# A two-layer hybrid trunk on one core: block-diagonal 128 by 128 products of the recurrent mixer rewritten as 64 by 64 products

## The chip, the cores and the metric

The kernel runs on one core of one Trainium2 chip. The metric is the device time of one execution in microseconds (us), as the median of several runs. The core has the matrix engine (TensorE, PE in the profile, with its weight loads listed apart as PEld), the vector engine (DVE), the scalar engine (ACT), GpSimd (POOL) and SyncE (SP), which here only starts transfers.

## The reference, cut to what matters

A trunk of two layers over 512 tokens of width 1024, all in float32. Layer 0 has a recurrent mixer of two kinds of heads, layer 1 block attention; both layers have an MLP and a gated side input. The change is in the second kind of heads of layer 0's mixer, eight heads of width 64 that carry a 64 by 64 state from token to token:

```python
def rwkv7_scan(r, decay, k, v, kk, a):
    def step(state, inp):
        r_t, w_t, k_t, v_t, kk_t, a_t = inp
        sa = jnp.einsum('bhvk,bhk->bhv', state, -kk_t)
        state = (state * w_t[:, :, None, :]
                 + sa[..., None] * (kk_t * a_t)[:, :, None, :]
                 + v_t[..., None] * k_t[:, :, None, :])
        return state, jnp.einsum('bhvk,bhk->bhv', state, r_t)
```

## The kernel before, in words

The two heads of a pair lie in the two halves of the 128 partitions, so there are four pairs (`hp`, 0 to 3). The kernel doesn't step through tokens. It cuts the 512 tokens into eight chunks of 64 and handles them in two groups (`g`) of four chunks; a group is two blocks (`a`) of two chunks (`c_`). For a pair and a group it does, in this order:

- `p1`: scores inside each chunk (line 600): the keys of one chunk as stationary operand, the queries of that chunk as moving operand. So that one product serves both heads, the keys are first copied by ACT into `BH`, a 128 by 128 tile that holds the two heads' 64 by 64 blocks on its diagonal and zeros elsewhere (line 596). DVE multiplies the products by a triangular mask into `NA` and `KA` (line 605). Then four transposes per block (line 614), whose results ACT copies into `TOK` and, one chunk at a time, into the halves of `BZ`, again with zeros around (line 619). Two further products (lines 625 and 631) follow.
- `p2`: a chain of products in float16 (line 664) that inverts a triangular matrix by doubling, each step waiting for a copy by ACT or DVE; it ends in `MU` (lines 690 and 693).
- `p3`: the maps of the state over one chunk. For each block one product with 256 moving columns (line 707) and two accumulated pairs with 128 (lines 710 and 711). DVE takes the map out of PSUM into `GB` (line 714), ACT the added state into `HS` (line 718). Then a chain over chunks (`states`, lines 744 and 746), woven with two products that use 64 columns of the array (`inner`, lines 726 and 731).

Steps are generators. `step` strings them together: in "A" `p2(h, 0)` is woven with the rest, in "C" `p2(h, 1)` is woven with `p3(h, 0)` and the next pair's `pre`. The large projections (`gemm`, lines 244 to 246, three products per operand pair) are written between them. All of it is put in order when the program is built, by a scheduler that sees priorities (`run` raises them by `OFS`). So what stands behind what in an engine's queue isn't read from the source but from the built program.

PSUM tiles of the mixer come from the ring `pmr` of four banks. Products with float32 operands appear in the profile as two passes each, with a weight load each: the 64 products of line 600 are 128 instructions there. The projections' operands are split beforehand into two float32r parts, and their products are one pass each.

Of the kernel before, what the change touches and what calls it, by code (L numbers as in the profile page):

```python
# [185 lines left out]
def trunk(ctx, tc, wts, xT, pT, vecs, lora, cst, lev, seg, rope, gain, out, upto="all", dbg=None, mode=None):  # L186
# [177 lines left out]
    def layer0_mixer(actp):  # L364
        ph = ExitStack()
        mp = ph.enter_context(tc.tile_pool(name="mp", bufs=1))
        BH = mp.tile([P, 2, 4, P], F32, name="BH")
        NAs = [mp.tile([P, 2, 2, 2, P], F32, name=f"NA{i}") for i in range(2)]
        KAs = mp.tile([P, 2, 2, 2, P], F32, name="KA")
        BZ = [mp.tile([P, 2, 2, 2, P], F32, name=f"BZ{i}") for i in range(2)]  # L370
        GB = mp.tile([P, 4, P], F32, name="GB")
        SB = mp.tile([P, 9, P], F32, name="SB")
        PP = mp.tile([P, 4, P], F16, name="PP")
        early = [BH, KAs, *NAs, *BZ, GB, SB, PP]
        for t in early[:NE]:
            G.memset(t, 0.0)
        nc.gpsimd.dma_start(cs, cst[:, :NKEEP])
# [206 lines left out]
            yield  # L584

        pk = [(a, h) for a in range(2) for h in range(2)]

        def p1(hp, g):
            lw, bh, kh, ar, rh_, bo, dl, v, y = pre_[hp]
            gs = slice(g * 256, g * 256 + 256)  # L590
            NA, KA, TOK = NAs[g], KAs, []
            un[hp, g] = (NA, TOK)

            for n, (src, dst) in enumerate(((bh, NA), (kh, KA))):
                for h in range(2):
                    A.copy(BH[hs[h], n, :, hs[h]], src[hs[h], gs].rearrange("p (c t) -> p c t", t=64))
                ps = pmr.tile([P, S], F32, name="pmr")
                for c_ in range(4):
                    o = g * 256 + c_ * 64
                    T.matmul(ps[:, c_ * P:c_ * P + P].rearrange("p (x t) -> p x t", x=2), BH[:, n, c_, :],  # L600
                             ar[:, :, o:o + 64], start=True, stop=True)
                pv = ps.rearrange("p (a c x t) -> p a c x t", a=2, c=2, x=2)
                for h in range(2):
                    for c_ in range(2):
                        V.tensor_tensor(dst[hs[c_], :, h, :, hs[c_]], pv[hs[h], :, c_, :, :],
                                        tri[hs[h], None, :, :].to_broadcast([64, 2, 2, 64]), op=OP.mult)
                yield
            for a in range(2):
                j = 2 * g + a
                js = slice(j * P, j * P + P)  # L610

                ps = pmr.tile([P, S], F32, name="pmr")
                for n, src in enumerate((ar[:, 0, :], v, bh, kh)):
                    T.transpose(ps[:, n * P:n * P + P], src[:, js], ident)
                t = E("TOK", 4, [P, 3, P])
                pv = ps.rearrange("p (x f) -> p x f", x=4)
                A.copy(t[:, 0:2, :], pv[:, 0:2, :])
                for c_ in range(2):
                    A.copy(BZ[g][hs[c_], a, :, c_, :], pv[hs[c_], 2:4, :])
                TOK.append(t)  # L620
                yield

            ps = pmr.tile([P, S], F32, name="pmr")
            for i, (a, h) in enumerate(pk):
                T.matmul(ps[:, i * 64:i * 64 + 64], KA[:, a, h, 0, :], TOK[a][:, 1, hs[h]], start=True, stop=True)
            for a in range(2):
                A.copy(TOK[a][:, 2, :], ps[:, a * P:a * P + P])
            yield
            ps = pmr.tile([P, S], F32, name="pmr")
            for i, (a, h) in enumerate(pk):  # L630
                T.matmul(ps[hs[h], a * P:a * P + P], TOK[a][:, 1, hs[h]], KA[:, a, h, 1, :], start=True, stop=True)
            A.copy(y[:, gs], ps[:, :256])
            yield
# [64 lines left out]
        def p3(hp, g):  # L698
# [2 lines left out]
            gs = slice(g * 256, g * 256 + 256)  # L701

            HS = E("HS", 1, [P, 4, 64])
            for a in range(2):
                bz = BZ[g][:, a]
                ps = pmr.tile([P, S], F32, name="pmr")
                T.matmul(ps[:, :256], MU[:, a, 0, :], bz[:, 0].rearrange("p c f -> p (c f)"), start=True, stop=True)
                for c_ in range(2):
                    o = ps[:, 256 + c_ * P:256 + c_ * P + P]
                    T.matmul(o, bz[:, 0, c_, :], MU[:, a, 1, :], start=True, stop=False)  # L710
                    T.matmul(o, bz[:, 1, c_, :], TOK[a][:, 1, :], start=False, stop=True)
                pv = ps.rearrange("p (x c f) -> p x c f", x=2, c=2)
                for h in range(2):
                    V.tensor_tensor(GB[hs[h], 2 * a:2 * a + 2, hs[h]], pv[hs[h], 0, :, hs[h]],
                                    cc("istack")[hs[h], None, :].to_broadcast([64, 2, 64]), op=OP.add)
                    for c_ in range(2):
                        ch = 4 * g + 2 * a + c_
                        A.activation(HS[hs[h], 2 * a + c_, :], pv[hs[h], 1, c_, hs[h]], AF.Copy,
                                     scale=dl[hs[h], ch:ch + 1])
                yield  # L720


            def inner():
# [618 lines left out]
```

## Time and profile before

| what | value |
|---|---|
| median of 3 runs | 1512.53 us (1509.21 to 1513.5) |
| the profiled execution | 1513.45 us |
| its span, first to last instruction | 1511.7 us |
| PE busy | 1484.5 us, 98% of the span |
| DVE, ACT, POOL busy | 932.4, 663.0, 137.9 us |
| mean granted TensorE clock | 0.993 |

The profile is one execution; its time is 0.92 us above the median, and its span leaves out 1.75 us ahead of the first and behind the last instruction. A busy PE isn't a full PE: the profile counts a matmul from its start to its modelled end, and matmuls overlap. What a product costs PE is read from the distance between starts. Layer 0's mixer with its projections lies from about 17 to 440 us.

### The profile page before, as it was taken

The numbers are of one execution on the slowest core, as the hardware profiler recorded it, in microseconds if no ns is written. First come the engines' busy times: TensorE is split into PE (matmuls) and PEld (weight loads), VectorE is DVE, ScalarE is ACT, GpSimd is POOL, SyncE is SP. The second block draws the span as 40 slices with busy tenths as digits, with TensorE's granted clock in tenths as the row PEclk, the third lists the DMA queues.
The fourth block names the chain that finished last, engine by engine and source line by source line (L and its number), as shares of the span: only waits on it lengthen the run. The fifth ranks groups of instructions, "written<-read, shape, count | busy, mean of one in ns | idle before, by whom it ended". The sixth has DMA issues, their size and how long they took to land.

```text
span 1511.7 us, 20553 instructions
## 1 busy us (share of the span) xinstructions
PE 1484.5 (98%) x7578; PEld 1199.8 (79%) x7578; DVE 932.4 (62%) x1831; ACT 663.0 (44%) x1269; POOL 137.9 (9%) x133
## 2 busy tenths in 40 slices
PE   9999999999999999999999999999999999999998
PEld 7678787777677888888888888777778888888887
DVE  6878697687775664444446648477575444445463
ACT  4575555554436433333334534454634333333342
POOL 4121220310205000000000200000220000000000
PEclk9999999999999999999999999999999999999999
DMA  5110111201123233333333432221123333333331
GB/s 179 56 36 22 55 43 44 67 29 49 36 91 105 91 98 98 98 98 94 97 96 98 131 115 83 78 63 49 55 79 97 92 104 98 98 95 95 98 98 70
DMA packets 67110, 123.88 MB, mean 82 GB/s; under 512 B 7633, under 2 KB 8017, under 8 KB 67009
## 3 DMA queue, kind: packets, MB, share of 16 engines
q1 hardware_dynamic: 65376, 118.57, 25.8%
q10 hardware_dynamic: 1152, 2.43, 0.5%
q0 software_dynamic: 480, 1.57, 0.3%
q8 instruction: 59, 0.97, 0.3%
q14 instruction: 43, 0.34, 0.1%
HBM read 120.45 MB, written 2.10 MB: 81 GB/s over the span
## 4 chain that ended last, share of the span: by engine, by line
PE 90%; DVE 5%; ACT 3%; issue 2%; DMA 1%; POOL 0%; SPq 0%; ACTq 0%; DVEq 0%; POOLq 0%
PE pj L244 21%; PE pj L246 20%; PE pj L245 20%; PE pmr L245 1%; PE pmr L246 1%; PE pmr L244 1%; PE pmr L1268 1%; PE pmr L1244 1%; PE pmr L664 1%; PE pj L1171 1%; PE pmr L1171 1%; PE pj L1173 1%; PE pmr L1173 1%; PE pmr L1172 1%; PE pj L1172 1%
## 5 line engine op out<-in xcount | busy, mean ns | idle before, releaser
L236 ACT CAST whi<-wr 128x512 fp32r<-128x512 f32 x428 | 264.8, 621 | 553.4 <-PE pj L245 424.6
L237 DVE TENSOR_TENSOR wlo<-wr,whi 128x512 fp32r<-128x512 f32 x428 | 309.9, 726 | 200.0 <-ACT whi L236 195.5
L244 PE MATMUL pj<-act,whi 128*128 128x512 f32 (+1 forms) x856 | 338.7, 397 | 1.2 <-DVE h L930 1.0
L246 PE MATMUL pj<-act,wlo 128*128 128x512 f32 (+1 forms) x856 | 336.5, 394 | 0.5 <-DVE wlo L237 0.5
L245 PE MATMUL pj<-act,whi 128*128 128x512 f32 (+1 forms) x856 | 336.9, 395 | 0.0
L244 PE MATMUL pj<-hid,whi 128*128 128x512 f32 x512 | 199.2, 389 | 0.0
L245 PE MATMUL pj<-hid,whi 128*128 128x512 f32 x512 | 199.2, 389 | 0.0
L246 PE MATMUL pj<-hid,wlo 128*128 128x512 f32 x512 | 199.2, 389 | 0.0
L244 PEld LDWEIGHTS pj<-act,whi 128*128 128x128 f32 x856 | 161.4, 189 | 34.8 <-issue 1.7
L246 PEld LDWEIGHTS pj<-act,wlo 128*128 128x128 f32 x856 | 161.3, 188 | 32.8 <-DVE wlo L237 1.5
L245 PEld LDWEIGHTS pj<-act,whi 128*128 128x128 f32 x856 | 161.4, 189 | 31.8 <-issue 2.0
L1110 DVE TENSOR_TENSOR x<-x,pj 128x512 f32<-128x512 f32 x128 | 88.0, 687 | 80.6 <-PE pj L246 80.2
L246 PEld LDWEIGHTS pj<-hid,wlo 128*128 128x128 f32 x512 | 96.1, 188 | 20.1
L245 PEld LDWEIGHTS pj<-hid,whi 128*128 128x128 f32 x512 | 96.1, 188 | 20.0
L244 PEld LDWEIGHTS pj<-hid,whi 128*128 128x128 f32 x512 | 96.1, 188 | 19.8
L319 POOL TENSOR_TENSOR acc<-acc,xsq 128x512 f32<-128x512 f32 x35 | 48.2, 1376 | 631.3 <-ACT xsq L313 612.7
L1099 DVE SCALAR_TENSOR_TENSOR r<-pj,rb 128x512 f32<-128x512 f32 x56 | 38.7, 691 | 84.0 <-PE pj L246 84.0
L278 DVE TENSOR_TENSOR hid<-r,hid 128x512 fp32r<-128x512 f32 x64 | 44.3, 692 | 41.5 <-ACT hid L277 41.4
L1100 ACT ACTIVATE r<-r 128x512 f32<-128x512 f32 x64 | 40.5, 632 | 21.6 <-DVE r L1099 21.5
L277 ACT CAST hid<-r 128x512 fp32r<-128x512 f32 x64 | 39.8, 621 | 1.9
L280 ACT ACTIVATE act<-x,vec 128x512 fp32r<-128x512 f32 x32 | 22.9, 720 | 30.4 <-DVE x L1128 12.7
L281 DVE SCALAR_TENSOR_TENSOR act<-x,vec,act 128x512 fp32r<-128x512 f32 x32 | 26.2, 836 | 8.6 <-ACT act L280 8.5
(388 smaller groups left out, 2244.2 us busy)
## 6 DMA issues: line engine op xcount, KB each, us to landing
wr<-in_wts_dram SPq DMA_DIRECT2D x428, 256.0 KB, 2.7
x<-in_xT_dram SPq DMA_DIRECT2D x8, 256.0 KB, 6.3
sr<-in_wts_dram SPq DMA_DIRECT2D x8, 256.0 KB, 5.2
out_dram<-x SPq DMA_DIRECT2D x7, 256.0 KB, 2.0
r<-in_pT_dram ACTq DMA_DIRECT2D x4, 256.0 KB, 2.7
lw<-in_lora_dram POOLq DMA_DIRECT2D x4, 192.0 KB, 3.1
tq<-in_rope_dram ACTq DMA_DIRECT2D x1, 512.0 KB, 5.1
tk<-in_rope_dram ACTq DMA_DIRECT2D x1, 512.0 KB, 6.0
```

The source lines that it names most:

```text
L236: A.copy(hi, raw)
L237: V.tensor_sub(lo, raw, hi.bitcast(F32))
L244: T.matmul(ps, wh, xh, start=first, stop=False)
L245: T.matmul(ps, wh, xl, start=False, stop=False)
L246: T.matmul(ps, wl, xh, start=False, stop=last)
L277: A.copy(h, src)
L278: V.tensor_sub(l, src, h.bitcast(F32))
L319: G.tensor_add(self.t, self.t, sq)
L1099: V.scalar_tensor_tensor(r, q, 0.0, nf[0], op0=OP.max, op1=OP.mult)
L1100: A.activation(r, r, AF.Square)
L1110: V.tensor_add(x[k], x[k], ps)
L1171: T.matmul(ps[j], xh, wh, start=k == 0, stop=False)
```

## The change

The zero-padded tiles go away. `BH` and its copies are dropped; `BZ` loses its chunk dimension, half its size, and is filled by one copy per block instead of two. Line 600 becomes 16 products per pair and group in place of 8, each with 64 rows and 64 columns of the array, so that one of the four quarters of the array (row half by head, column half by chunk) does one head and one chunk. The three kinds of products in `p3` become 24 of 64 by 64 with 64 moving columns in place of 10 of 128 by 128. Two PSUM banks are used at a time, one per row half. The mask step, the map into `GB` and the scaling into `HS` have the same counts and sizes. `p1` and `p3` hand back control at other points (`yield`).

```diff
--- before.py
+++ after.py
@@ -364,14 +364,13 @@
     def layer0_mixer(actp):
         ph = ExitStack()
         mp = ph.enter_context(tc.tile_pool(name="mp", bufs=1))
-        BH = mp.tile([P, 2, 4, P], F32, name="BH")
         NAs = [mp.tile([P, 2, 2, 2, P], F32, name=f"NA{i}") for i in range(2)]
         KAs = mp.tile([P, 2, 2, 2, P], F32, name="KA")
-        BZ = [mp.tile([P, 2, 2, 2, P], F32, name=f"BZ{i}") for i in range(2)]
+        BZ = [mp.tile([P, 2, 2, P], F32, name=f"BZ{i}") for i in range(2)]
         GB = mp.tile([P, 4, P], F32, name="GB")
         SB = mp.tile([P, 9, P], F32, name="SB")
         PP = mp.tile([P, 4, P], F16, name="PP")
-        early = [BH, KAs, *NAs, *BZ, GB, SB, PP]
+        early = [KAs, *NAs, GB, SB, PP]
         for t in early[:NE]:
             G.memset(t, 0.0)
         nc.gpsimd.dma_start(cs, cst[:, :NKEEP])
@@ -584,6 +583,7 @@
             yield
 
         pk = [(a, h) for a in range(2) for h in range(2)]
+        quads = [(c_, h) for c_ in range(2) for h in range(2)]
 
         def p1(hp, g):
             lw, bh, kh, ar, rh_, bo, dl, v, y = pre_[hp]
@@ -591,20 +591,21 @@
             NA, KA, TOK = NAs[g], KAs, []
             un[hp, g] = (NA, TOK)
 
-            for n, (src, dst) in enumerate(((bh, NA), (kh, KA))):
-                for h in range(2):
-                    A.copy(BH[hs[h], n, :, hs[h]], src[hs[h], gs].rearrange("p (c t) -> p c t", t=64))
-                ps = pmr.tile([P, S], F32, name="pmr")
-                for c_ in range(4):
-                    o = g * 256 + c_ * 64
-                    T.matmul(ps[:, c_ * P:c_ * P + P].rearrange("p (x t) -> p x t", x=2), BH[:, n, c_, :],
-                             ar[:, :, o:o + 64], start=True, stop=True)
-                pv = ps.rearrange("p (a c x t) -> p a c x t", a=2, c=2, x=2)
+            pq = [pmr.tile([P, S], F32, name="pmr").rearrange("p (n a x t) -> p n a x t", n=2, a=2, x=2)
+                  for h in range(2)]
+            for n, src in enumerate((bh, kh)):
+                for a in range(2):
+                    for c_, h in quads:
+                        o = g * 256 + a * P + c_ * 64
+                        T.matmul(pq[h][hs[c_], n, a], src[hs[h], o:o + 64], ar[hs[h], :, o:o + 64],
+                                 start=True, stop=True)
+            yield
+            for n, dst in enumerate((NA, KA)):
                 for h in range(2):
                     for c_ in range(2):
-                        V.tensor_tensor(dst[hs[c_], :, h, :, hs[c_]], pv[hs[h], :, c_, :, :],
-                                        tri[hs[h], None, :, :].to_broadcast([64, 2, 2, 64]), op=OP.mult)
-                yield
+                        V.tensor_tensor(dst[hs[c_], :, h, :, hs[c_]], pq[h][hs[c_], n],
+                                        tri[hs[c_], None, :, :].to_broadcast([64, 2, 2, 64]), op=OP.mult)
+            yield
             for a in range(2):
                 j = 2 * g + a
                 js = slice(j * P, j * P + P)
@@ -615,8 +616,7 @@
                 t = E("TOK", 4, [P, 3, P])
                 pv = ps.rearrange("p (x f) -> p x f", x=4)
                 A.copy(t[:, 0:2, :], pv[:, 0:2, :])
-                for c_ in range(2):
-                    A.copy(BZ[g][hs[c_], a, :, c_, :], pv[hs[c_], 2:4, :])
+                A.copy(BZ[g][:, a], pv[:, 2:4, :])
                 TOK.append(t)
                 yield
 
@@ -701,23 +701,29 @@
             gs = slice(g * 256, g * 256 + 256)
 
             HS = E("HS", 1, [P, 4, 64])
+            bz = BZ[g]
+            pq = [pmr.tile([P, S], F32, name="pmr")[:, :256].rearrange("p (a x f) -> p a x f", a=2, x=2)
+                  for c_ in range(2)]
             for a in range(2):
-                bz = BZ[g][:, a]
-                ps = pmr.tile([P, S], F32, name="pmr")
-                T.matmul(ps[:, :256], MU[:, a, 0, :], bz[:, 0].rearrange("p c f -> p (c f)"), start=True, stop=True)
-                for c_ in range(2):
-                    o = ps[:, 256 + c_ * P:256 + c_ * P + P]
-                    T.matmul(o, bz[:, 0, c_, :], MU[:, a, 1, :], start=True, stop=False)
-                    T.matmul(o, bz[:, 1, c_, :], TOK[a][:, 1, :], start=False, stop=True)
-                pv = ps.rearrange("p (x c f) -> p x c f", x=2, c=2)
+                for c_, h in quads:
+                    T.matmul(pq[c_][hs[h], a, 0], MU[hs[c_], a, 0, hs[h]], bz[hs[c_], a, 0, hs[h]],
+                             start=True, stop=True)
+                for c_, h in quads:
+                    T.matmul(pq[c_][hs[h], a, 1], bz[hs[c_], a, 0, hs[h]], MU[hs[c_], a, 1, hs[h]],
+                             start=True, stop=False)
+                for c_, h in quads:
+                    T.matmul(pq[c_][hs[h], a, 1], bz[hs[c_], a, 1, hs[h]], TOK[a][hs[c_], 1, hs[h]],
+                             start=False, stop=True)
+            yield
+            for c_ in range(2):
                 for h in range(2):
-                    V.tensor_tensor(GB[hs[h], 2 * a:2 * a + 2, hs[h]], pv[hs[h], 0, :, hs[h]],
+                    V.tensor_tensor(GB[hs[h], c_::2, hs[h]], pq[c_][hs[h], :, 0],
                                     cc("istack")[hs[h], None, :].to_broadcast([64, 2, 64]), op=OP.add)
-                    for c_ in range(2):
-                        ch = 4 * g + 2 * a + c_
-                        A.activation(HS[hs[h], 2 * a + c_, :], pv[hs[h], 1, c_, hs[h]], AF.Copy,
-                                     scale=dl[hs[h], ch:ch + 1])
-                yield
+            for a in range(2):
+                for c_, h in quads:
+                    ch = 4 * g + 2 * a + c_
+                    A.activation(HS[hs[h], 2 * a + c_, :], pq[c_][hs[h], a, 1], AF.Copy, scale=dl[hs[h], ch:ch + 1])
+            yield
 
 
             def inner():
```

How this moves work on PE shows in the built program. First place: PE in step "C" of the third pair, where `p3(2, 0)` begins. Rows are the line, the product, out<-in by the program's names, and out rows x moving columns; "x4" is four in a row; L244 to L246 are the projection's products. Before:

```order
L707 MATMUL pmr<-BZ_108,MU 128x256
L710 MATMUL pmr<-MU,BZ_108 128x128
L711 MATMUL pmr<-TOK,BZ_108 128x128
L244 MATMUL pj<-act,whi 128x512
L710 MATMUL pmr<-MU,BZ_108 128x128
L245 MATMUL pj<-act,whi 128x512
L711 MATMUL pmr<-TOK,BZ_108 128x128
L246 MATMUL pj<-act,wlo 128x512
```

With the change:

```order
L709 MATMUL pmr<-BZ_107,MU 64x64 x3
L244 MATMUL pj<-act,whi 128x512
L709 MATMUL pmr<-BZ_107,MU 64x64
L712 MATMUL pmr<-MU,BZ_107 64x64
L245 MATMUL pj<-act,whi 128x512
L712 MATMUL pmr<-MU,BZ_107 64x64
L246 MATMUL pj<-act,wlo 128x512
L712 MATMUL pmr<-MU,BZ_107 64x64
L244 MATMUL pj<-act,whi 128x512
L712 MATMUL pmr<-MU,BZ_107 64x64
L245 MATMUL pj<-act,whi 128x512
L715 MATMUL pmr<-TOK,BZ_107 64x64
```

A projection product stands between one small product and the next in both, and there are now more small products to stand between. Second place: PE at `p3(3, 1)`, the last maps of the mixer. Before:

```order
L707 MATMUL pmr<-BZ_109,MU 128x256
L710 MATMUL pmr<-MU,BZ_109 128x128
L711 MATMUL pmr<-TOK,BZ_109 128x128
L710 MATMUL pmr<-MU,BZ_109 128x128
L711 MATMUL pmr<-TOK,BZ_109 128x128
L707 MATMUL pmr<-BZ_109,MU 128x256
```

With the change:

```order
L709 MATMUL pmr<-BZ_108,MU 64x64 x4
L712 MATMUL pmr<-MU,BZ_108 64x64 x4
L715 MATMUL pmr<-TOK,BZ_108 64x64 x4
L709 MATMUL pmr<-BZ_108,MU 64x64 x4
L712 MATMUL pmr<-MU,BZ_108 64x64 x4
L715 MATMUL pmr<-TOK,BZ_108 64x64 x4
```

Here nothing stands between them, in either program. Third place: PE at `p1(0, 1)`. Before:

```order
L519 MATMUL pmr<-id_91,XT 128x128
L600 MATMUL pmr<-ar,BH 128x128 x4
L664 LDWEIGHTS n_603
L664 MATMUL pmr<-X,n_603 128x64
```

With the change:

```order
L518 MATMUL pmr<-id_91,XT 128x128
L245 MATMUL pj<-act,whi 128x512
L600 MATMUL pmr<-ar,bh 64x128 x8
L600 MATMUL pmr<-ar,kh 64x128 x8
L625 MATMUL pmr<-TOK,KA 128x64 x3
```

The scores of both operands are now one run of 16, where the four products of the second operand used to follow some rows later. In the whole changed program the new products stand in 68 unbroken runs: 11 of line 600 (five of 16 products, and three groups of 16 split as 2 and 14 or 1 and 15), and 57 of lines 709 to 715. Of the 57, 48 stand between two projection products; 43 of these hold one product, four hold two, one holds eight. The other nine hold 3, 3, 12, 12, 12, 19, 24, 24 and 24. Of the products of lines 726 and 731 (732 and 737 in the change), eight stand singly beside projection products before; after, four do, and the other four stand in one run.

## Rows read from the trace of the kernel before

**Rows 1.** The page: engines' busy time, and the chain that ended last.
```profile
PE 1484.5 (98%) x7578; PEld 1199.8 (79%) x7578; DVE 932.4 (62%) x1831; ACT 663.0 (44%) x1269; POOL 137.9 (9%) x133
...
PE 90%; DVE 5%; ACT 3%; issue 2%; DMA 1%; POOL 0%; SPq 0%; ACTq 0%; DVEq 0%; POOLq 0%
```

**Rows 2.** Busy time by stretch; behind the engines the granted clock, DMA share, GB/s.
```profile
60.00:420.00 360.00, 351.31 (x2534) 279.04 (x2533) 273.75 (x651) 194.15 (x443) 66.56 (x66) 1.00 0.14 42
```

**Rows 3.** Groups by line and form, PE: array rows*columns, moving size, count | busy, mean ns.
```profile
L600 PE MATMUL pmr<-ar,BH 128*128 128x128 f32 x128 | 17.5, 281 | 0.0
...
L711 PE MATMUL pmr<-TOK,BZ 128*128 128x128 f32 x64 | 12.3, 274 | 0.0
L710 PE MATMUL pmr<-MU,BZ 128*128 128x128 f32 x64 | 12.3, 274 | 0.0
...
L707 PE MATMUL pmr<-BZ,MU 128*128 128x256 f32 x32 | 10.4, 407 | 0.3 <-ACT MU L693 0.3
```

**Rows 4.** Timeline, PE, p1(0, 0): start us, us, instruction, count.
```profile
64.40 1.95 PE L600 MATMUL pmr<-ar,BH 128*128 128x128 f32 x16
66.18 0.27 PE L614 MATMUL pmr<-cs,ar 128*128 128x128 f32 x1
```

**Rows 5.** Timeline, PE, 371 to 381 us: products between projection products.
```profile
371.28 0.59 PE L707 MATMUL pmr<-BZ,MU 128*128 128x256 f32 x2
371.52 0.58 PE L245 MATMUL pj<-act,whi 128*128 128x512 f32 x1
371.94 0.38 PE L710 MATMUL pmr<-MU,BZ 128*128 128x128 f32 x2
372.08 0.48 PE L246 MATMUL pj<-act,wlo 128*128 128x512 f32 x1
372.40 0.38 PE L711 MATMUL pmr<-TOK,BZ 128*128 128x128 f32 x2
...
373.76 0.39 PE L244 MATMUL pj<-act,whi 128*128 128x512 f32 x1
373.99 0.40 PE L245 MATMUL pj<-act,whi 128*128 128x512 f32 x1
...
378.18 0.43 PE L726 MATMUL pmr<-NA,MU 128*64 128x128 f32 x2
378.55 0.49 PE L244 MATMUL pj<-act,whi 128*128 128x512 f32 x1
378.97 0.43 PE L726 MATMUL pmr<-NA,MU 128*64 128x128 f32 x2
```

**Rows 6.** Timeline, PE, an unbroken group of line 726.
```profile
110.07 0.29 PE L664 MATMUL pmr<-X,n 128*128 128x64 f16 x4 [0.18 <-DVE X L669]
110.29 0.66 PE L726 MATMUL pmr<-NA,MU 128*64 128x128 f32 x8
110.88 0.55 PE L851 MATMUL pmh<-qs,KS 128*128 128x64 f32 x3
```

**Rows 7.** Timeline, PE, four float16 products.
```profile
71.32 0.28 PE L664 MATMUL pmr<-X,n 128*128 128x64 f16 x4
71.44 0.86 PE L625 MATMUL pmr<-TOK,KA 128*128 128x64 f32 x6
```

**Rows 8.** Lines 596 and 619: durations min/median/max, and who waited for line 619.
```profile
L596 ACT COPY BH<-kh x16: 387/402/406, 58.3 to 330.6; 64x256 f32<-64x256 f32 x16
L596 ACT COPY BH<-bh x16: 388/403/407, 63.1 to 329.6; 64x256 f32<-64x256 f32 x16
...
L619 ACT COPY BZ<-pmr x32: 361/367/370, 68.2 to 350.9; 64x256 f32<-64x256 f32 x32
...
  PE pmr L631: 1.2, 2
```

**Rows 9.** Timeline, POOL, at the start: the memsets and the first sum.
```profile
0.74 0.95 POOL L376 MEMSET BH<- 128x1024 f32 x1 [0.29 <-POOLq L1331]
...
5.03 1.86 POOL L379 MEMSET BZ<- 128x1024 f32 x2
...
9.03 1.32 POOL L414 TENSOR_TENSOR sq<-sq 128x512 f32<-128x512 f32 x1 [0.21 <-ACT sq L411]
```

**Rows 10.** Timeline, PE, the end of the mixer.
```profile
433.58 0.60 PE L334 MATMUL pmh<-cs,rs_on 128*128 128x128 f32 x4
433.93 0.48 PE L245 MATMUL pj<-os,whi 128*128 128x512 f32 x1
434.25 0.40 PE L246 MATMUL pj<-os,wlo 128*128 128x512 f32 x1
438.03 0.80 PE L244 MATMUL pj<-os,whi 128*128 128x512 f32 x1 [3.38 <-ACT os L277]
```

## Prediction

> **What bounds the kernel now.** I read the page first, then the busy time of the mixer's stretch, then single starts on PE. PE is busy for 98% of the span and makes 90% of the chain that ended last [rows 1]. [...] The reader is to see that the projections fill PE whenever the mixer's chain waits. So a change here is worth what it adds to or takes from PE's queue, and ACT's saved copies are worth only what PE waits for them.
>
> The mean durations of the groups [rows 3] can't be multiplied: they are latencies of overlapping passes. Starts can. The sixteen passes of line 600 start at 64.40 and the next product at 66.18, so a full-array pass of 128 columns takes 1.78 / 16 = 0.111 us of PE [rows 4]. Between projection products the same holds: one stands 0.23 us before the next (373.76, 373.99), and a product of line 710 (two passes) makes the period 372.40 - 371.94 = 0.46, so it adds 0.23 us. A product of line 707 (256 columns) makes it 371.94 - 371.28 = 0.66 and adds 0.43, 0.216 per pass [rows 5].
>
> The nearest relative of the new products is line 726, whose products use 64 columns of the array, alternating between its two halves. Two things show. First, halves work at the same time: eight passes and the way out take 110.88 - 110.29 = 0.59 us [rows 6]; eight in a row at 0.109 would need 0.87. Four turns of two passes give 0.44; the other 0.15 is the first turn's load and the way out. The way in takes some 0.09 more: the four float16 products before it start 0.03 apart [rows 7], so the last began at 110.16 and the next could have at 110.19. An unbroken run thus costs 0.24 us on top of its turns. Second, a single product between projection products is dear: 378.97 - 378.18 = 0.79, less 0.23, is 0.56 us, where its two passes fill 0.22 [rows 5]. So 0.34 goes for changing the array's division twice. Line 710 in the same position pays next to nothing.
>
> **The change, part by part.** Removed from PE: 128 passes of line 600 and 128 of lines 710 and 711 at 0.111 us, 14.2 each, and 32 of line 707 at 0.216, 6.9 (counts [rows 3]). Together 35.3 us.
>
> Added by line 600: 128 products of two passes. If four quarters work at once, that is 64 turns of 128 columns, and 6 more because three groups are split: 70 x 0.109 = 7.6 us. The 11 runs cost 11 x 0.24 = 2.6, and 0.2 more for two that begin behind a projection product. Sum 10.4.
>
> Added by lines 709 to 715: no row shows a pass of 64 moving columns on a quarter. I take half of 0.109, 0.055 us a turn. The 48 runs between projection products pay 0.34 each; 47 of them need two turns (0.45 each, 21.2 us), the one with eight products four (0.56). The other nine runs have 68 turns (3.7 us), 9 x 0.24 = 2.2 and 0.4 for the four behind a projection product. Sum 28.1. So the new products cost 38.5 us, and the exchange adds **3.2 us** to PE. The saving of the unbroken runs is eaten by the single ones, whose quarter can't share the array with another.
>
> The scheduler also moves others. Eight products of lines 726 and 731 beside projection products cost about 4.4 us before; now four cost 2.2 and a run of four 0.8. I take -1.4.
>
> What bounds the new price: quarters might be fed no faster than the closest starts of short products I find, 0.03 us apart [rows 7], against 0.055 / 4 = 0.014 in a full turn. The nine long runs and the run of eight hold some 140 products, 280 passes: 280 x 0.014 = +3.9 us at most; line 600's turns give 0.027 and change little. I keep 0.014, because pairs of line 726 already share a turn, and leave 3.9 for the range. [...]
>
> ACT loses 32 copies of 0.40 us into `BH` and half of the 32 of 0.37 into `BZ` [rows 8], 18.7 us. The projections on PE hide nearly all of this already, since ACT has half its time free. PE waited 1.2 us in two waits for `BZ` ahead of line 631 [rows 8]; with one copy fewer in each of these waits I take -1. The two mask steps and the map keep their sizes on DVE, which I cost at nothing; their cover is the projections, and without it a mask step late by one product costs 0.4. POOL loses three memsets of 0.95; the first sum behind them waits 0.21 for ACT already [rows 9], and no engine waits for POOL there: nothing.
>
> At the end PE stands 3.38 us, waiting for the last split (`os`), shortly behind the transposes of line 334 [rows 10]. In the changed order a dozen projection products more follow these transposes before the queue needs that split. They can fill up to 2.8 us, but only if they weren't needed to fill another gap before. I take -1, with 0 and -3 as ends. Against it, `p3` of the first group stretches: in the third pair 24 products over 21 runs with projection products between take 20 x 0.68 = 14 us, where ten took 10 x 0.46 and a bit. The queue of `p2`'s chain stands behind that. I take +1, between 0 and +6; two banks of `pmr` held at once belong to the same term.
>
> Sum: 3.2 - 1.4 - 1 - 1 + 1 = +0.8 us. The profiled execution took 1513.45, giving 1514.2; it lay 0.9 above the median, so against the median I forecast **1513 us**: no change. A measurement of this kernel can tell about 0.3%, 4.5 us, from nothing.
>
> **Rivals.** *Row halves don't share a turn* (slower). Rows show column halves side by side, never row halves, since every product before uses all 128 rows. If only columns pair up, line 600 needs 17.2 us and lines 709 to 715 32.0, 10.7 more: 1524 us. It is decided by whether products of line 600 start in fours or in twos. For it: nothing shows the contrary. Against: passes already bypass one another between column halves, and the change gives each row half a bank of its own. Chance 0.20. [...] If no quarter shared with another, it would be 32 more, 1545 us: 0.05, against line 726's pairs.
>
> *Late maps* (slower). The stretched `p3` delays `p2` and the last chain, which has no projection left behind it: +6 and no gain at the end gives 1521. For it: `p3(3, 0)` is stretched too, ahead of the mixer's end. Against: PE is full there, and the projection products done meanwhile aren't lost. 0.09.
>
> *Fewer waits* (faster). The end's stall goes (-3.4), the waits for ACT copies go with it, and stretching costs nothing: 1507 us. ACT is rid of a tenth of its work in the stretch, 18.7 of 194 us. Against: most of PE's waits are for others. 0.17.
>
> *Changing the division is nearly free for quarters*, as it is for line 710: 48 x 0.34 and 20 x 0.24 fall away, 21 us: 1492 us. Against it line 726 speaks plainly [rows 5]. 0.06.
>
> **How the numbers follow.** The forecast has 0.43; its own range is 1508 to 1517, with the issue bound of 3.9 as its upper end. Faster by over 0.3% holds the two last rivals, 0.23; slower the first ones, 0.34. The range of 1504 to 1525 us takes in fewer waits and column pairs; it leaves out the case without sharing, most of the nearly free one, and little else.
>
> **What would show it.** In the changed profile, 16 products of line 600 in one run should take about 1.0 us from the first start to the next line's; 1.9 to 2 would be column pairs, 3.6 none. The last 24 products of lines 709 to 715 should take some 0.8 us, 1.5 with a floor of 0.03 per pass. A single one between projection products should make the period 0.68; if it is near 0.35, the forecast is wrong on the fast side. PE's wait for `os` at the mixer's end should be between 0 and 3.4 us. Wrong altogether would be a mixer whose end moves by over 5 us while these four hold: then waits, which I cost at nearly nothing, decide.

## The result, and the profile after

The change made the kernel slower: **1525.68 us** (median of 4 runs, 1524.45 to 1528.07) against 1511.85 before (4 runs, 1509.21 to 1513.5), a ratio of 1.0094 with an interval of 1.0082 to 1.0107. The forecast was 1513 in a range of 1504 to 1525; the time lies 0.7 us outside it, and on the side that had a chance of 0.34. The profiled execution took 1525.49 us with a span of 1523.7 us.

From the page of the changed kernel: busy time of the engines, and the chain that ended last.

```profile
PE 1491.6 (98%) x7930; PEld 1191.5 (78%) x7930; DVE 934.4 (61%) x1831; ACT 645.6 (42%) x1221; POOL 137.4 (9%) x130
...
PE 88%; DVE 7%; issue 2%; ACT 2%; DMA 1%; POOL 0%; SPq 0%; DVEq 0%; ACTq 0%; POOLq 0%
```

Beside [rows 1], ACT lost 17.4 us (18.7 were counted), and DVE kept its work, yet DVE's share of the chain rose from 5 to 7%. Next the four things that the prediction said would decide. The PE timeline of the changed kernel (start us, us, instruction, count of passes; in brackets the wait ahead of it):

```profile
63.69 0.67 PE L600 MATMUL pmr<-ar,bh 64*64 64x128 f32 x16
64.18 0.62 PE L600 MATMUL pmr<-ar,kh 64*64 64x128 f32 x16
64.73 0.33 PE L615 MATMUL pmr<-cs,ar 128*128 128x128 f32 x1
...
97.09 0.32 PE L712 MATMUL pmr<-MU,BZ 64*64 64x64 f32 x2
97.35 0.49 PE L244 MATMUL pj<-act,whi 128*128 128x512 f32 x1
97.77 0.33 PE L712 MATMUL pmr<-MU,BZ 64*64 64x64 f32 x2
...
115.97 0.28 PE L664 MATMUL pmr<-X,n 128*128 128x64 f16 x4 [2.22 <-DVE X L669]
...
136.98 0.33 PE L709 MATMUL pmr<-BZ,MU 64*64 64x64 f32 x4
...
137.82 0.43 PE L625 MATMUL pmr<-TOK,KA 128*128 128x64 f32 x2
...
414.85 1.08 PE L857 MATMUL pmh<-qs,KS 128*128 128x64 f32 x8 [1.27 <-DVE KS L853]
416.38 1.35 PE L857 MATMUL pmh<-qs,KS 128*128 128x64 f32 x8 [0.45 <-DVE KS L853]
...
429.51 0.35 PE L709 MATMUL pmr<-BZ,MU 64*64 64x64 f32 x8
...
430.37 0.49 PE L890 MATMUL pmh<-h 128*128 128x128 f32 x2
...
448.90 0.63 PE L334 MATMUL pmr<-cs,bc 128*128 128x128 f32 x4 [2.00 <-DVE bc L330]
453.31 0.73 PE L244 MATMUL pj<-os,whi 128*128 128x512 f32 x2 [1.52 <-ACT os L277]
```

The sixteen products of line 600 take 64.73 - 63.69 = 1.04 us, so four quarters share a turn (forecast 1.0). The last 24 products of lines 709 to 715 take 430.37 - 429.51 = 0.86 (forecast 0.8, and 1.5 with an issue floor). A single one between projection products has a period of 97.77 - 97.09 = 0.68, exactly the forecast. The wait for `os` is 1.52, inside the 0 to 3.4. All four hold, and the time is wrong all the same. Among the waits in the middle of the list, the 2.22 us for DVE at 115.97 are new. The 1.27 and 0.45 us for `KS` have counterparts in other kernels, as shown below.

Where they come from shows in the busy time by stretch of the changed kernel (us, length, busy time and count of PE, PEld, DVE, ACT, POOL; then the granted clock, DMA share, GB/s):

```profile
60.00:420.00 360.00, 347.87 (x2752) 261.10 (x2752) 265.00 (x628) 174.09 (x386) 67.38 (x66) 0.99 0.13 42
...
95.00:101.20 6.20, 6.20 (x41) 3.41 (x37) 0.00 (x0) 1.32 (x3) 0.62 (x1) 1.00 0.00 1
101.20:107.00 5.80, 5.57 (x60) 4.18 (x59) 5.58 (x12) 4.05 (x10) 0.00 (x0) 1.00 0.14 48
107.00:113.00 6.00, 6.00 (x44) 5.09 (x45) 5.37 (x15) 4.05 (x10) 2.58 (x4) 1.00 0.14 44
113.00:116.00 3.00, 0.78 (x8) 0.66 (x8) 2.91 (x8) 1.56 (x3) 2.45 (x3) 1.00 0.00 0
...
269.20:283.10 13.90, 13.90 (x72) 7.70 (x69) 3.20 (x6) 2.68 (x7) 1.23 (x2) 1.00 0.12 39
283.10:300.00 16.90, 16.70 (x84) 12.37 (x83) 10.80 (x20) 11.31 (x22) 2.61 (x3) 1.00 0.20 62
...
375.50:386.50 11.00, 11.00 (x65) 6.13 (x64) 3.17 (x7) 2.11 (x4) 0.62 (x1) 1.00 0.13 48
400.00:410.00 10.00, 9.21 (x79) 6.74 (x76) 9.45 (x19) 7.59 (x14) 2.49 (x2) 1.00 0.19 55
410.00:417.00 7.00, 5.28 (x45) 4.59 (x44) 7.00 (x13) 3.72 (x11) 5.52 (x5) 1.00 0.12 37
417.00:427.30 10.30, 10.30 (x54) 9.73 (x53) 6.63 (x13) 2.43 (x5) 1.91 (x2) 0.50 0.01 2
```

and in the kernel before:

```profile
95.00:101.20 6.20, 6.20 (x43) 5.01 (x43) 4.99 (x11) 3.87 (x11) 2.17 (x3) 1.00 0.17 44
...
113.00:116.00 3.00, 3.00 (x32) 2.33 (x31) 2.92 (x8) 0.37 (x1) 1.11 (x2) 1.00 0.00 0
...
396.00:412.00 16.00, 13.74 (x106) 11.29 (x106) 15.18 (x27) 9.15 (x21) 8.95 (x8) 1.00 0.07 21
```

From 95 to 101.2 us PE strings the first pair's single products between projection products. PE is full, and DVE does nothing at all, where in before it is busy for 4.99 us. From 101.2 to 113 DVE is all but full; from 113 to 116 PE is busy for 0.78 of 3 us, because DVE is behind. Over the whole 360 us PE is busy for 347.87 us, where before had 351.31 [rows 2].

The later pairs don't repeat this. The third pair has the longest stretch: from 269.2 to 283.1 us DVE works only 3.20 of 13.9 us, and yet PE stands for only 0.2 us in the 16.9 that follow. In the last pair DVE works 3.17 of 11 us in the stretch and 16.45 of 17 from 400 to 417, and PE stands 17 - 14.49 = 2.5 us there; but before has 2.3 us of it in the like place, from 396 to 412, with DVE busy for 15.18 of 16. What differs there is the clock: from 417.0 to 427.3 us the granted clock is 0.50, the lower of the two levels in these traces (the upper is 1.00), with PE busy throughout; ahead of the fall PE had been busy for 5.28 of 7 us. In before the clock falls to 0.50 later and for less time, from 437.2 to 444.0 us.

DVE's side of it, first its timeline in the changed kernel, where the bracket says how long DVE had been idle and for whom:

```profile
101.28 0.69 DVE L488 TENSOR_TENSOR u<-pj,rb 128x512 f32<-128x512 f32 x1 [8.29 <-PE pj L246]
...
109.38 1.18 DVE L267 TENSOR_TENSOR ra_kk<-rs_kk 128x8 f32<-128x8 f32 x1
...
115.48 0.44 DVE L669 CAST_PREDICATED X<-m,pmr 128x256 f16<-128x256 uint8 x1
```

POOL's timeline in the same place:

```profile
109.34 1.19 POOL L570 TENSOR_TENSOR ar<-r,pd 128x512 f32<-128x512 f32 x1
```

and DVE's in the kernel before:

```profile
95.69 0.28 DVE L714 TENSOR_TENSOR GB<-pmr,cs 64x128 f32<-64x128 f32 x1 [3.41 <-PE pmr L711]
...
99.61 0.69 DVE L489 TENSOR_TENSOR u<-pj,rb 128x512 f32<-128x512 f32 x1 [0.43 <-PE pj L246]
...
107.17 0.17 DVE L267 TENSOR_TENSOR ra_kk<-rs_kk 128x8 f32<-128x8 f32 x1
```

In before DVE reaches `u` 1.7 us earlier, and its longest idle time there is 3.41 us, not 8.29. And part of the full DVE in the changed kernel isn't work. Small instructions on 128x8, which take 0.17 us in before, take 1.18, 1.00, 1.15 and 0.60 us ahead of `X`, and each of them ends within 0.05 us of the end of a POOL instruction on 128x512. That is 3.3 us more, and the PE wait for `X` behind them is 2.22: without these 3.3 us `X` would have come in time. Which of the two makes the hole, the late start or the neighbourhood of POOL, the other kernels tell (below, behind the seventh).

The sums of DVE's waits from 60 to 440 us (total, times, longest), in the changed kernel:

```profile
DVE GB L720 <- PE pmr L715: 19.1, 11, 4.6
...
DVE u L488 <- PE pj L246: 10.0, 3, 8.3
DVE SB L752 <- PE pmr L750: 7.1, 10, 2.1
```

and in the kernel before:

```profile
DVE GB L714 <- PE pmr L711: 11.5, 11, 3.4
...
DVE SB L746 <- PE pmr L744: 2.6, 5, 1.9
...
DVE u L489 <- PE pj L246: 2.2, 3, 0.9
```

DVE waits 7.6 us more for the maps, 7.8 more for the projections that `u` is read from, through which the singles are threaded, and 4.5 more for the state's step behind the maps. Other waits of DVE fell, those for `X` from 11.0 to 4.1 and those for `h` of one projection from 10.5 to 7.0 us, so these sums alone don't say what reached PE.

To put sizes on this I split PE's time. Up to the start of the 1200th projection product I added the distances from one PE start to the next. The distance that a product has where nothing disturbs it is PE's work; what is over is a wait, time lost to the lower clock included. These sums are worked out from all PE rows of each profiled execution.

| kernel | 1200th projection product, us | PE's work | waits | median us |
|---|---|---|---|---|
| before | 523.96 | 470.3 | 52.4 | 1511.85 |
| the change | 536.59 | 471.6 | 63.7 | 1525.68 |

Behind that product both take the same (987 to 988 us). So of 12.6 us, **PE's work brings 1.3 and waits bring 11.3**. The lower clock explains part of the waits: 11.0 us of them were lost at 0.50 after, 5.9 before; so 5.1 of the 11.3 are clock and 6.2 are PE standing.

Two other readings agree. The idle time that the profile shows ahead of PE's instructions, added up to the same product, is 20.5 us before and 25.6 after, 5.1 more. Of these, 2.3 lie between the 200th and the 300th projection product, where the hole at 113 us is; the rest comes in pieces below 1 us per hundred products, and what makes those isn't shown. And span times mean granted clock, for each execution on record, estimates the span that it would have at the upper level: the medians are 1502.6 us in before (the same for the 19 and for the 13 executions beside the experiments) and 1510.2 in the change. The clock is on record to 0.001, which is 1.5 us of a span. So by this estimate some 7.6 of the 13.8 us would stay without the lower clock, and the clock costs about 6.2.

### The profile page after: what moved, and what is told of

Its sections match the earlier page's. It is cut to its first block, busy times and chain, and to the rows that moved or that the text cites. A ratio compares the mean times of both kernels' runs of the same rounds, so it can differ in the third digit from the quotient of the medians.

```text
span 1523.7 us, 21214 instructions
## 1 busy us (share of the span) xinstructions
PE 1491.6 (98%) x7930; PEld 1191.5 (78%) x7930; DVE 934.4 (61%) x1831; ACT 645.6 (42%) x1221; POOL 137.4 (9%) x130
## 4 chain that ended last, share of the span: by engine, by line
PE 88%; DVE 7%; issue 2%; ACT 2%; DMA 1%; POOL 0%; SPq 0%; DVEq 0%; ACTq 0%; POOLq 0%
PE pj L244 20%; PE pj L246 20%; PE pj L245 20%; PE pmr L1274 1%; PE pmr L1250 1%; PE pmr L245 1%; DVE wlo L237 1%; PE pmr L246 1%; PE pmh L857 1%; PE pmr L244 1%; PE pj L1177 1%; PE pmr L1177 1%; PE pj L1179 1%; PE pmr L1179 1%; PE pmr L1178 1%
## 5 line engine op out<-in xcount | busy, mean ns | idle before, releaser
L236 ACT CAST whi<-wr 128x512 fp32r<-128x512 f32 x428 | 265.1, 622 | 569.2 <-PE pj L245 422.9
L237 DVE TENSOR_TENSOR wlo<-wr,whi 128x512 fp32r<-128x512 f32 x428 | 313.6, 735 | 201.6 <-ACT whi L236 193.6
L244 PE MATMUL pj<-act,whi 128*128 128x512 f32 (+1 forms) x856 | 340.7, 399 | 1.5 <-DVE h L936 1.0
L246 PE MATMUL pj<-act,wlo 128*128 128x512 f32 (+1 forms) x856 | 338.1, 396 | 0.8 <-DVE wlo L237 0.8
L244 PE MATMUL pj<-hid,whi 128*128 128x512 f32 x512 | 199.2, 389 | 0.0
L246 PE MATMUL pj<-hid,wlo 128*128 128x512 f32 x512 | 199.2, 389 | 0.0
L244 PEld LDWEIGHTS pj<-act,whi 128*128 128x128 f32 x856 | 161.6, 189 | 36.6 <-issue 2.0
L246 PEld LDWEIGHTS pj<-act,wlo 128*128 128x128 f32 x856 | 161.6, 189 | 34.3 <-DVE wlo L237 1.9
L246 PEld LDWEIGHTS pj<-hid,wlo 128*128 128x128 f32 x512 | 96.1, 188 | 20.0
L244 PEld LDWEIGHTS pj<-hid,whi 128*128 128x128 f32 x512 | 96.1, 188 | 19.9
```

Of the source, the lines that this page charges most:

```text
L236: A.copy(hi, raw)
L237: V.tensor_sub(lo, raw, hi.bitcast(F32))
L244: T.matmul(ps, wh, xh, start=first, stop=False)
L246: T.matmul(ps, wl, xh, start=False, stop=last)
```

## Experiments

The theory (S): the prices on PE are as forecast, and the loss comes from the maps' 24 small products per group, which the order strings out between projection products. Two rivals: the scores' two banks and their late masks bring the waits, and the maps cost only their share of PE (Q); any new order of the queues costs some waits, wherever the change is (R). After the first four kernels a second pair of theories was tried: late maps (L; the loss comes because what needs the maps gets them late) and slow service (B; while PE alternates between singles and projections, everything else that DVE and ACT need from PE also comes late).

**1. The scores alone.** Line 600 as changed, with its mask step and without `BH`; `BZ` and `p3` as before.

```diff
-                    T.matmul(ps[:, c_ * P:c_ * P + P]..., BH[:, n, c_, :], ar[:, :, o:o + 64], ...)
+                        T.matmul(pq[h][hs[c_], n, a], src[hs[h], o:o + 64], ar[hs[h], :, o:o + 64], ...)
```

> The scores of the change (line 600 on quarters, no BH), the maps of the kernel before. On PE 14.2 us of full products go and 10.4 come: -3.8. Theory S (the loss is waits that the stretched maps bring, 43 products standing singly between projection products): no added wait here, so 3 to 5 us faster than before, about 1508. Rival Q (the scores' two banks and their late masks bring the waits): 5 to 10 us slower than before. Rival R (any new order of the queues costs some waits, wherever the change is): 0 to 8 us slower.

Measured: 1511.22 us (10 runs, 1509.15 to 1512.66), before on the same chip 1512.58 (19 runs); ratio 0.9991, 0.9981 to 1.0. PE's work is 467.7, 2.6 less than before, waits 51.1. This speaks against Q, which gave 5 to 10 us slower, and R's 0 to 8 slower only touches the interval. The gain of 1.4 us is smaller than the 3 to 5 that S gave: the scores barely help.

**2. The maps alone.** `p1` and `BH` as before; `BZ`, lines 709 to 715 and the copies behind them as changed.

```diff
-                T.matmul(ps[:, :256], MU[:, a, 0, :], bz[:, 0].rearrange("p c f -> p (c f)"), ...)
+                for c_, h in quads:
+                    T.matmul(pq[c_][hs[h], a, 0], MU[hs[c_], a, 0, hs[h]], bz[hs[c_], a, 0, hs[h]], ...)
```

> The maps of the change (lines 709 to 715 on quarters), the scores of the kernel before. By the built order 46 runs, 35 of them one product between projection products: about 23.3 us for 21.1 on PE, +2 to +4 with runs whose quarters pair only in twos. Theory S: waits as in the change, 8 to 14 us slower than before. Rival Q: 2 to 4 us slower, PE's share alone. Rival R: 5 to 12 slower, and the waits elsewhere than at the maps.

Measured: 1523.17 us (4 runs, 1520.65 to 1526.46); ratio 1.0063, 1.0043 to 1.0082. The loss is the maps': 10.6 us slower, out of Q's range, but inside both S's and R's, which this run doesn't tell apart. PE's work is 470.4 as before (470.3), the waits are 65.5, 13.1 more, in a profiled execution that was the slowest of the four (1526.46).

**3. The maps' products lifted.** The changed kernel, with a higher priority for the maps' products alone, so that nothing is put between them.

```diff
+PUP = 600
...
-            for a in range(2):
-                for c_, h in quads:
+            with tc.high_priority(offset=PUP):
+                for a in range(2):
+                    for c_, h in quads:
```

> The change with the maps' products at a higher priority, so that each group of 24 is one run of the queue (19 runs in place of 68). By the prices that the change's trace confirms, PE needs 20.7 us less than in the change. Theory S: the waits of the change, some 11 us, go as well, most of them: 1495 to 1499, faster than before by 13 to 17 us. Rival Q or R: the waits stay: 1503 to 1507, 5 to 9 us faster than before. Slower than before would refute the prices themselves.

Measured: **1500.02 us** (4 runs, 1499.21 to 1501.39); ratio to before 0.9916, 0.9901 to 0.9931. That is 25.7 us less than the change, and faster than both kernels. PE's work is 455.2 and the waits 54.5: 16.4 and 9.2 less than with the change, 25.6 together. The 12.6 us gained on before lie between the two expectations, just short of S's 13 to 17 and well beyond the 5 to 9 of Q and R; PE's work fell by less than the 20.7 worked out. And part of the 9.2 is clock: up to the 1200th projection product the clock was at the lower level for 6.8 us, in the change for 23.9, while PE's idle time there is 21.8, 3.8 less. Span times clock (median 1489.8) is 20.4 us below the change, 12.8 below before: so without the clock the waits that go are some 4 us, and the gain on before is no matter of the clock. The PE timeline of this kernel at `p3(0, 0)`, where the change has its first singles (lines stand one or two further down here):

```profile
95.43 0.34 PE L711 MATMUL pmr<-BZ,MU 64*64 64x64 f32 x8
...
96.06 0.30 PE L717 MATMUL pmr<-TOK,BZ 64*64 64x64 f32 x8
96.29 0.26 PE L665 MATMUL pmr<-X,n 128*128 128x64 f16 x3
```

and its busy time by stretch, columns as above:

```profile
60.00:420.00 360.00, 348.77 (x2936) 267.97 (x2935) 281.62 (x684) 180.60 (x404) 67.36 (x66) 1.00 0.14 42
...
95.00:101.20 6.20, 6.20 (x89) 4.57 (x88) 4.17 (x12) 5.12 (x14) 0.62 (x1) 1.00 0.03 9
...
113.00:116.00 3.00, 2.94 (x31) 1.98 (x30) 2.92 (x9) 0.99 (x2) 1.06 (x1) 1.00 0.05 19
```

The 24 products take 96.29 - 95.43 = 0.86 us, where those of the change are strung out over more than 6. DVE works 4.17 of the 6.2 us in which it had nothing, and PE's hole from 113 to 116 is gone. At the end of this kernel's mixer PE still waits for `KS`, in three waits of 0.95, 0.45 and 0.61 us, so those waits aren't what the change lost.

**4. The same lift in the kernel before.** Lines 707 to 711 of before under the same priority.

```diff
+                with tc.high_priority(offset=PUP):
+                    T.matmul(ps[:, :256], MU[:, a, 0, :], bz[:, 0].rearrange("p c f -> p (c f)"), ...)
```

> The kernel before with the same higher priority for its own maps' products; nothing else changes. Full-array products between projection products cost nothing extra, so PE's work stays. Theory S: within 3 us of before, either way. Rival R: a new order, 0 to 8 us slower. If it is faster by 5 us or more, the priority itself is the gain, and e3 shows nothing of quarters.

Measured: 1514.01 us (10 runs, 1510.79 to 1517.51); ratio 1.0009, 1.0 to 1.0019. The priority alone gains nothing; it pays only for products on quarters. This fits [rows 5], where line 710 between projection products adds 0.46 - 0.23 = 0.23 us, about twice the 0.111 of a full-array pass [rows 4].

**5. Early maps, and idle singles in their old place.** The lifted kernel, and in the first group of each pair 24 more products on quarters at the old priority, which nobody reads.

```diff
+            if g == 0:
+                xq = [pmr.tile([P, S], F32, name="pmr")... for c_ in range(2)]
+                for a in range(2):
+                    for x in range(3):
+                        for c_, h in quads:
+                            T.matmul(xq[c_][hs[h], a, x % 2], MU[hs[c_], a, 0, hs[h]], bz[hs[c_], a, 0, hs[h]], ...)
```

> The maps early and in one run as in e3_maps_up, and in the place where they stood in the change 24 quarter products per pair (first group only) that nothing reads, at the old priority. They spread between the projection products as the maps of the change do (66 runs, 38.5 us by the confirmed prices, 20.6 more than e3_maps_up). Theory L (the change's waits come from late maps: what needs them is held back): the maps are early here, so PE's 20.6 us alone, 1519 to 1522. Theory B (they come from PE serving the other engines slowly in that stretch, after which DVE and ACT are behind): the waits return, some 10 us more, 1528 to 1533.

Measured: 1527.71 us (4 runs, 1524.3 to 1530.22); ratio to before 1.0104, 1.0086 to 1.0122. That is beyond L's range and 0.3 us short of B's. The maps come as early as in the third kernel, and still it is 27.7 us slower than that one, where the added products are priced at 20.6 on PE. In the profiled executions PE's work is 18.8 larger and the waits 5.4. The clock isn't in these 5.4: up to the 1200th projection product it was at the lower level for 6.8 us in both, and PE's idle time is 27.0 us for 21.8. DVE's timeline of this kernel shows that it starves without any map being late,

```profile
102.26 0.69 DVE L489 TENSOR_TENSOR u<-pj,rb 128x512 f32<-128x512 f32 x1 [4.56 <-PE pj L247]
```

the PE timeline that PE then waits for DVE,

```profile
117.95 0.28 PE L665 MATMUL pmr<-X,n 128*128 128x64 f16 x4 [2.28 <-DVE X L670]
```

and the busy time by stretch the turn from one to the other:

```profile
100.00:105.00 5.00, 4.77 (x46) 3.11 (x46) 2.35 (x5) 1.35 (x2) 0.00 (x0) 1.00 0.06 16
...
115.00:120.00 5.00, 2.72 (x16) 2.10 (x16) 4.92 (x14) 2.75 (x5) 1.39 (x2) 0.95 0.00 0
```

So nearly the same wait, 2.28 us for 2.22, stands at the same place with maps that are early. That excludes L for this wait. Here too small instructions on DVE beside POOL's are stretched ahead of it, up to 1.12 us. The idle products, like the maps in the change, hold two `pmr` banks until the last one is done; but in the execution PE doesn't stand for a bank in the stretch (busy for 6.20 of 6.20 us in the change; here its one wait from 100 to 105 is 0.23 us for DVE's `u`), and the 2.2 us are waits for `X`, an operand. Whether the banks shaped the built order isn't kept apart.

**6. The lift for the last pair alone.** `offset=PUP if hp == 3 else 0`.

> As e3_maps_up, but the raised priority for the last pair of heads alone; 49 runs, by the confirmed prices 11.1 us more than e3_maps_up. If the change's waits sit at the end of the mixer, where no projection is left behind the last pair: 1510 to 1513. If each stretched group brings its own share of them: 1514 to 1518.

Measured: 1513.97 us (10 runs, 1512.38 to 1518.29); ratio 1.0018, 1.0008 to 1.0028. The 11.7 us below the change lie between the two expectations. In the profiled execution, which was 3.0 us above the median, PE's work fell by only 3.5 us, where the built order gives 9.6, and the waits by 5.2 to 58.5, though the clock was at the lower level from 409.2 to 422.9. Between the two theories the run doesn't decide. Averaged over all executions the granted clock is 0.994 here, as in the third kernel, and 0.991 to 0.993 in the change and in the second and fifth kernels, where the last pair's products are strung out too. As far as four executions of each of those tell, the clock's share thus belongs to the last pair.

**7. The lift for lines 732 and 737 too.** The third kernel, with the same priority around the products of `inner`.

> As e3_maps_up, and the products of lines 732 and 737 (halves of the array, read by the inner outputs) at the same raised priority, so that the last pair's four single ones stand in one run. PE saves 4 x 0.34 us: 1497 to 1500 if nothing else moves; up to 1504 if earlier inner products hold back the chain of states.

Measured: 1499.43 us (4 runs, 1496.78 to 1501.4); ratio 0.9917, 0.9902 to 0.9933. That is as expected, but it can't be told from the third kernel: PE's work is 2.8 less and its waits 5.3 more (59.8), in a profiled execution that had the lower clock for 20.5 us up to the 1200th projection product, against 6.8 there.

**The path, over all kernels.** B says that PE's hole in the first pair comes from DVE starving in the stretch of singles. The timelines speak against it. In the second kernel the first pair's maps happen to be one unbroken run, and `u` comes at 98.49; yet PE waits 1.56 us for `X`, behind small DVE instructions of 1.23 and 1.19 us that end with POOL's:

```profile
93.56 0.34 PE L709 MATMUL pmr<-BZ,MU 64*64 64x64 f32 x8
...
114.98 0.28 PE L664 MATMUL pmr<-X,n 128*128 128x64 f16 x4 [1.56 <-DVE X L669]
```

The fourth kernel has no quarter products at all, and PE waits for `X` in the same place, behind a small DVE instruction that ends with a POOL instruction (115.02 and 114.99 us):

```profile
113.79 1.23 DVE L270 SCALAR_TENSOR_TENSOR rs_kk<-ra_kk,rs_kk 128x8 f32<-128x8 f32 x1
...
115.41 0.28 PE L665 MATMUL pmr<-X,n 128*128 128x64 f16 x4 [1.17 <-DVE X L670]
```

And in the sixth kernel the first pair's singles are strung out as in the change and DVE starves for 6.82 us, but PE doesn't wait for `X` at all:

```profile
99.17 0.44 DVE L670 CAST_PREDICATED X<-m,pmr 128x256 f16<-128x256 uint8 x1 [6.82 <-PE pmr L665]
```

So the hole goes with where the small DVE instructions come to lie beside POOL's, which any new order can move, and not with the starving. R thus holds in part: PE's idle time up to the 1200th projection product is 20.5 us in before, 21.8 to 24.2 in the first, third, fourth, sixth and seventh kernels, and 25.6, 27.6 and 27.0 in the change, the second and the fifth, which string out the last pair's products too. Some 1 to 4 of the change's 5 us are no more than other new orders cost.

## Why the prediction was wrong

**The single prices on PE held, their sums only roughly.** Four quarters shared a turn (1.04 us for line 600's 32 passes), a single cost 0.34 over its share (a period of 0.68), a full run had no issue floor of 0.03 a pass (0.86 us for 48). The forecast of exchange and regrouping, 3.2 - 1.4 = +1.8, came out as +1.3 of PE's work, and that is in part luck. Runs that hold only two products of each line at a time fill turns half: the run of twelve at 136.98 takes 0.84 us, as long as 24 at 429.51. Such runs cost 1.8 more in all, and one run of line 600 whose two operands came interleaved 0.45. And the other kernels don't follow their own sums well: the scores alone took 2.6 off PE's work where 3.8 were worked out, the maps alone left it as it was where their built order gave +2.2, and the lift of all maps took off 16.4 where 20.7 were worked out. Other products are placed elsewhere when these move; which ones wasn't followed up.

**The step that failed** is the one on the stretch: "I take +1, between 0 and +6", with the gains beside it, "-1" for the `BZ` waits and "-1, with 0 and -3 as ends" at the end. Together they were -1; measured are **+11.3 us**: 6.2 of PE standing, and 5.1 of lower clock, for which the sum had no term. The prediction named the stretch of `p3` (14 us in the third pair; 95 to 101.2 us is the first pair's), but asked only who waits for `p3`, namely `p2`'s chain. It didn't ask what DVE and ACT have to do while PE spends its time on singles. A projection product came every 0.23 us [rows 5], every 0.46 around a product of line 710, and comes every 0.68 in the stretch. In the first pair DVE stood 8.29 us behind that. But the starving isn't what cost PE its time: the third pair's long stretch, which the prediction had in mind, brought PE next to no waits, and the hole of 2.2 us in the first pair stands where small DVE instructions had moved beside POOL's. "The two mask steps and the map keep their sizes on DVE, which I cost at nothing; their cover is the projections" was true of their sizes, but a new order moves other instructions of DVE as well, and for that the sum had nothing. What makes the remaining 4 us of standing is open.

**The gains went elsewhere.** The waits of 1.2 us for `BZ` are gone, but PE waits 1.2 for DVE's `KA` at line 625. At the end the 3.38 for `os` [rows 10] became 1.52, and line 334 waits 2.00 for `bc` just before. Both terms are nil.

**The rivals.** "Row halves don't share", 1524 us, came closest in time, and is excluded by line 600's starts (1.04 us, where it gave 1.9 to 2). "Late maps" gave 1521 (its own terms, +6 for +1 and 0 for -1, give 1519), and it too had the stretch for its cause. Its own path, `p2` behind `p3`, isn't what decides in the first pair: with early maps the wait is there all the same. The prediction's last sentence held: the four signs stood and the end moved, so waits decided.

**The lower clock** had no term. Its share, 5.1 of the 11.3 us in the profiled execution, varies from run to run: the fifth kernel's profiled execution has the same waits for `KS` at the mixer's end and a clock of 1.00 from 390 to 440 us. Over all executions it is about 6.2 of the 13.8 us, by the estimate above. That the loss is the maps' is shown by the second kernel, and that it goes when their products are kept together by the third. That strung-out products bring the lower clock rests on the averages given with the sixth alone (0.991 to 0.993, against 0.994), and by what path they make PE stand is open; B isn't borne out.

## What to carry to other kernels

When an edit splits few large products into many small ones, look in the built order for where they land: here a run with something else between its products paid 0.34 us for each change of the array's division and back. And allow for waits: a new order of the queues alone moved PE's idle time by 1 to 4 us here, and the clock by more, which a sum of prices doesn't show. An engine that falls idle in the stretch looks like the cause, but it has to be followed to a wait of PE, in more than one kernel. If the small products can be kept together, as by the priority here, the exchange that lost 0.9% gains 0.8%.

## What the runs showed of the hardware

Averaged over a run, quarters are fed faster than any short products in the trace of before. In the last run of the changed kernel 48 passes of 64 columns take 0.86 us from the first start to the next product's, 0.018 us a pass, where four float16 products in a row started 0.03 apart [rows 7]. Single starts were closer already in before, which the prediction overlooked: neighbouring passes of lines 631, 726 and 731, which alternate between the column halves, start 0.005 to 0.007 us apart in some 80 places. So the 0.03 that the prediction took as a possible floor is none for passes on different quarters or halves.

The change of division and back had nearly the same price in the two divisions that the traces show: between projection products a single 64 by 64 product cost 0.45 us (0.68 - 0.23), one on 64 columns 0.56 [rows 5]. By the estimates of the forecast (0.055 and 0.109 us a pass, two passes each) 0.11 and 0.22 of these fill the array, so 0.34 is left in both. What PE does in these 0.34 us isn't seen in the rows.

Some small instructions of DVE ran longer beside POOL's. DVE instructions on 128x8 took 0.17 us with POOL idle (at 107.17 us in before) and, in the changed kernel, 0.60 to 1.18 beside POOL instructions on 128x512, and ended with them. Not every one did: in before one on 128x8 at 105.47 us took 0.17 beside the POOL instruction at 104.92. And POOL's weren't longer for it: that one took 1.18 us, the same one in the changed kernel, at 109.34, 1.19.
